# Two features of an output projection pinned behind the last attention score, and square sums of the last quarters moved between VectorE and GpSimd

## The chip, the cores and the metric

The kernel runs on one core of one Trainium2 chip. A core has TensorE (PE; its weight loads are listed apart as PEld), VectorE (DVE), ScalarE (ACT), GpSimd (POOL) and SyncE (SP, whose queue issues most transfers here). Each engine works through a queue of its own in order, and semaphores hold an instruction until those it depends on are done. The metric is device time in microseconds (us), as the median of several runs. Lower is better.

## The reference, cut to what matters

Two layers over 1024 latent tokens with 1024 features, with a prefix of 256 context tokens. The second layer, the only one that the change touches, is an odd layer: a conformer convolution (512 features) beside a neighbourhood attention (8 heads of 64), an output projection, a gated residual, and then the final norm:

```python
def odd_mixer(h_lat, h_ctx, w_in, w_out, ...):
    ...
    od = lax.map(d_row, (jnp.arange(rows), q_rows))          # neighbourhood attention
    od = jnp.moveaxis(od, 0, 1).reshape(bsz, n, D_W)
    y_lat = jnp.concatenate([oc, od * jax.nn.silu(dg)], axis=-1) @ w_out
    ...
x_lat = x_lat + g_l[:, None, :] * y_lat
return rms_norm(x_lat, final_g)      # x / sqrt(mean(x^2) + eps) * g
```

All values are 32-bit floats.

## The kernel before

**Products.** Every product of 32-bit data is made of three TensorE products: each operand is split in a high part (a cast on ScalarE, L312) and a low part (the rest, a subtraction on GpSimd or VectorE, L315), and `mm3` issues high by high (L332), high by low (L333) and low by high (L334). In names, `wh`/`wl` are the parts of a weight block, `wr` the block as it was transferred, `od` the parts of the gated attention output.

**Order.** The code is a set of generators. `weave` runs the attention (`main`) and lets steps of a second generator (`fill`) in between, in a ratio taken from the table `WV`. A scheduler then sets each engine's order from estimated times, and `tc.issue_after(x)` pins what is issued under it behind instruction `x`. So the order on an engine is not that of the code, and has to be read from the program.

**Attention of the second layer.** It is worked through in groups of one pair of heads by one half of the tokens (512). For each block of keys of a group: score (L509, L513, tile `st`), on most blocks the addition of a bias on VectorE (L518), exponential on ScalarE (L519 or, where there is no bias, L521; tile `pf`), split into `ph` and `pl`, and three products with the values (L460, L461, L462) that add up in `ov`. After the last block VectorE makes the reciprocal of the denominators (L470 transpose to `r`, L472, L473 transpose to `rb`), multiplies (L1337, tile `y`) and gates (L1339), and `y` is split once more (L312, L315) into the eighth block of 128 attention features of the output projection, `od` of that half. The last group belongs to the second half of the tokens. `sts` is the list of all score products; its last entry is the first score product (L509) of the last block.

**Output projection.** The 1024 inputs of the projection are eight blocks f = 0 to 7 of 128; f = 0 to 3 come from the convolution, f = 4 to 7 from the attention. Outputs are eight blocks too (e = 0 to 7, "features" below), for the two halves of tokens. What is ready early is added early: `out1_part` makes the product of the given blocks `fs` for halves `ks` and adds it, times the gate, to the residual (L1409, `x` += `po` * `modT`). It goes over pairs of features (`e2`), whose weights it loads first (`load_w`: transfer, cast, split). One call is for f = 4, 5, 6 of the second half (k = 1): per feature, nine products of 512 columns. `out1_end(k)` finishes a stretch of tokens: k = 0 is the first half (f = 4 to 7), k = 1 and k = 2 are the third and the fourth quarter (256 columns each, f = 7 alone).

**Square sums and norm.** For each finished feature `out1_end` squares it on ScalarE (L1438). The squares of e = 0 and 1 are the two accumulators, and those of e = 2 to 7 are added to them (L1442): even ones to the first, odd ones to the second. The table `SQP` says per k which of these adds run on GpSimd; the others run on VectorE. For k = 2 the two accumulators are added too (L1445). `rstd_steps` sums them over partitions on TensorE (L259, `trs`), adds epsilon (L262, `rbv`), takes the power -1/2 on GpSimd (L246, `nr`) with one refining step on VectorE (L247 to L249), and spreads the result over partitions (L269, `bc`). `final_norm` copies that to SBUF (L1453, `bcs`) and scales the features: those in `FNP[k]` on ScalarE and GpSimd (L1457, L1458), the others on VectorE (L1460), and sends pairs of them out (L1462).

Of the kernel before, what the change touches and what calls it, by code (L numbers as in the profile page):

```python
# [54 lines left out]
LAG = (6, 6, 6, 12)  # L55
FIN = (2, 2)
WV = (77, 45, 85, 24, 12)
# [4 lines left out]
ADDS = (0, 0, 1)  # L62
BCT = ("mx", "st", "mx")
FNP = ((0, 1, 2, 3, 4, 5, 6), (0, 2, 4, 6), (6,))
SQP = ((2, 3, 4, 5, 6), (), (4, 6))
ENDS = ((0, 0, 512), (1, 0, 256), (1, 256, 256))
LATE = 100
GB = 2
# [20 lines left out]
def tile_kernel(ctx: ExitStack, tc: tile.TileContext, a, out):  # L89
# [12 lines left out]
    sts = []  # L102
# [169 lines left out]
    @contextmanager  # L272
    def later(n):

        p = tc.cur_priority
        tc.cur_priority = p + n
        yield
        tc.cur_priority -= n

    def run(gen):  # L280

        while True:
            try:
                next(gen)
            except StopIteration as e:
                return e.value
# [255 lines left out]
    def weave(main, nmain, fill, nfill, last=True, all_fill=True, lag=0):  # L542

        done = 0
        for k in range(nmain):
            next(main, None)
            while done * nmain < (k + 1) * nfill:
                with ExitStack() as cx:
                    cx.enter_context(later(FL[layer[0]]))
                    if lag and len(sts) >= lag:  # L550
                        cx.enter_context(tc.issue_after(sts[-lag].ins))
                    next(fill, None)
                done += 1
        if all_fill:
            for _ in fill:
                pass
        if last:
            for _ in main:
                pass
# [133 lines left out]
    with ExitStack() as p0x:  # L693
# [208 lines left out]
        main = attn_gen(a0, [group0(u, qb) for u in ORDER for qb in QORD], VS0, LOOK0)  # L902
# [117 lines left out]
    with ExitStack() as l1x:  # L1020
# [357 lines left out]
        def x2_load(e):  # L1378
            for c in range(2):
                x2_of[e, c] = half("xs", "hf")  # L1380
                SC.dma_start(x2_of[e, c], X1[:, e, c * 512 : (c + 1) * 512])

        def od_load(hf):
            od[hf] = bigp.tile([P, 2, 3, 512], F32R, tag="big", name=nm("od"))
            for f in range(3):
                split(yo[:, f, hf], od[hf][:, 0, f, :], od[hf][:, 1, f, :], "s", ODE)
# [21 lines left out]
                x = x2[k][:, e, o : o + n]  # L1408
                VE.scalar_tensor_tensor(x, pp, scale, x, op0=ALU.mult, op1=ALU.add)  # L1409

        def out1_part(fs, ks=(0, 1)):
            for e2 in range(4):
                w = load_w(wp, a["od_wo"], e2, 256, WB, dks=fs)
                for e in (2 * e2, 2 * e2 + 1):
                    if fs[0] == 0:
                        x2_load(e)
                    for k in ks:
                        yield from out1(fs, e, k, *w)
# [3 lines left out]
        def out1_end(k):  # L1422
# [3 lines left out]
            for e in range(DK):  # L1426
# [14 lines left out]
                else:  # L1441
                    (GP if e in SQP[k] else VE).tensor_tensor(accs[e % 2], accs[e % 2], sq, op=ALU.add)  # L1442
                yield
# [24 lines left out]
        def ends(evs):  # L1468
            for ev in evs:
                k = int(ev[1])  # L1470
                if ev[0] == "e":
                    yield from out1_end(k)
                elif ev[0] == "c":
                    bcs[k] = yield from rstd_steps(dpool, sums[k], ENDS[k][2], BCT[k])
                else:
                    yield from final_norm(k, bcs[k])

        main = attn_gen(dlow, groups1, VSH, LOOK1, {11: [], 12: [13, 14], 13: [15]})
# [4 lines left out]
        assert fin[0] >= 12  # L1483
        for hf in (1, 0):
            od_load(hf)
        weave(main, WV[3], out1_part((4, 5, 6), (1,)), 8, False, True, LAG[3])
        assert fin[0] >= 14
        weave(main, WV[4], ends(EV0), NEV, False, True)
        wend = load_end(wp, a["od_wo"], 7, 256, WB)
        run(main)  # L1490
        solo[0] = True
        run(ends(EVS))


# [120 lines left out]
```

## Time and profile before

| | |
|---|---|
| median of three runs | 1559.18 us (1559.18, 1565.87, 1557.75) |
| the profiled execution | 1559.91 us, of which the trace's span is 1558.1 us |
| busy share of the span | PE 94%, PEld 75%, DVE 67%, ACT 48%, POOL 51% |
| mean granted TensorE clock | 0.965 |
| the chain that ended last, by engine | PE 79%, DVE 13%, DMA 3% |

The page of the profile gives the busy time of each engine, the costliest groups of instructions, and the chain of work that ended last, followed back from the last instruction. TensorE is the busiest engine and carries most of the chain. Shares over the whole span hide that the end of the program looks different; its stretches are shown with the prediction. A row of the timeline gives start and duration in us, engine, line, operation, output and inputs by name, shape, and in brackets the idle time before it and what ended that.

### The profile page before, as it was taken

To read this page: it belongs to the slowest core of one execution; us is meant where nothing else is said; L and a number is where in the kernel's file an instruction comes from. 1 tells how busy PE (TensorE), PEld (TensorE's weight loads), DVE (VectorE), ACT (ScalarE), POOL (GpSimd) and SP (SyncE) were. 2 spreads that over 40 slices of the span, in tenths; PEclk is the share of its full clock that TensorE was granted. 3 is DMA by queue.
4 is the path that set the end of the run, shared out by engine and by line. 5 is a ranking of instruction groups with operands and counts; after the bars stand their busy time and mean duration, and the time that the engine had idled before them with its cause. 6 is when DMAs were issued, how large, how long until landed. Compare 5 with 4: busy or idle time off the path is not lost.

```text
span 1558.1 us, 21469 instructions
## 1 busy us (share of the span) xinstructions
PE 1459.1 (94%) x7084; PEld 1175.6 (75%) x7084; DVE 1050.0 (67%) x2113; ACT 746.9 (48%) x1418; POOL 801.5 (51%) x637
## 2 busy tenths in 40 slices
PE   6899999998998989999999878999999899989995
PEld 2786978896896768876866657888887688868875
DVE  2833557579579765466677846999756566577866
ACT  3721434444435564447556663443334355455563
POOL 3530434455445765557656664665632344364675
PEclk9899999999999999999999889999999899999996
DMA  9473315422312245121112012111445777878632
GB/s 366 161 244 124 108 57 181 143 70 92 119 51 79 92 151 177 54 68 50 51 31 92 7 34 86 58 55 41 142 159 192 216 204 236 263 227 243 183 111 108
DMA packets 154168, 199.83 MB, mean 128 GB/s; under 512 B 14716, under 2 KB 95816, under 8 KB 154056
## 3 DMA queue, kind: packets, MB, share of 16 engines
q1 hardware_dynamic: 147392, 186.88, 38.0%
q10 hardware_dynamic: 6664, 11.57, 2.3%
q8 instruction: 56, 0.92, 0.2%
q14 instruction: 56, 0.46, 0.1%
HBM read 148.07 MB, written 49.02 MB: 126 GB/s over the span
## 4 chain that ended last, share of the span: by engine, by line
PE 79%; DVE 13%; DMA 3%; issue 2%; ACT 2%; POOL 1%; SPq 0%; DVEq 0%; POOLq 0%; ACTq 0%
PE p L332 7%; PE p L333 7%; PE p L334 7%; PE ov L460 4%; PE ov L462 4%; PE ov L461 4%; PE st L509 4%; PE st L513 4%; PE po L333 4%; PE po L332 4%; PE po L334 4%; PE pq L332 3%; PE pq L334 3%; PE pq L333 3%; PE pm L184 2%
## 5 line engine op out<-in xcount | busy, mean ns | idle before, releaser
L315 POOL TENSOR_TENSOR pl<-pf,ph 128x512 fp32r<-128x512 f32 (+4 forms) x321 | 396.8, 1247 | 375.8 <-ACT ph L312 328.7
L521 ACT ACTIVATE pf<-st 128x512 f32<-128x512 f32 x284 | 166.3, 597 | 210.3 <-PE st L513 171.0
L315 POOL TENSOR_TENSOR wl<-wr,wh 128x512 fp32r<-128x512 f32 (+2 forms) x131 | 170.5, 1313 | 141.4 <-ACT wh L312 121.4
L312 ACT CAST ph<-pf 128x512 fp32r<-128x512 f32 (+4 forms) x364 | 209.2, 588 | 29.0 <-PE ov L461 16.7
L332 PE MATMUL p<-hh,wh 128*128 128x512 f32 x448 | 178.2, 398 | 5.3 <-ACT hh L312 2.8
L333 PE MATMUL p<-hl,wh 128*128 128x512 f32 x448 | 176.1, 394 | 0.6 <-POOL hl L315 0.6
L334 PE MATMUL p<-hh,wl 128*128 128x512 f32 x448 | 173.7, 394 | 0.0
L509 PE MATMUL st<-QH,KAt 128*128 128x512 f32 (+4 forms) x364 | 140.9, 388 | 8.9 <-ACT pf L521 8.1
L460 PE MATMUL ov<-ph,Vt 128*128 128x512 f32 (+4 forms) x364 | 142.5, 392 | 5.6 <-DVE y L670 4.3
L462 PE MATMUL ov<-pl,Vt 128*128 128x512 f32 (+4 forms) x364 | 141.9, 390 | 1.8 <-POOL pl L315 1.8
L461 PE MATMUL ov<-ph,Vt 128*64 128x512 f32 (+4 forms) x364 | 140.5, 386 | 0.0
L513 PE MATMUL st<-QL,KBt 68*128 68x512 f32 (+4 forms) x364 | 136.4, 386 | 2.0 <-DVE QL L438 2.0
L1085 DVE SCALAR_TENSOR_TENSOR cps<-U,taps,cps 128x512 f32<-128x512 f32 x184 | 126.4, 751 | 0.9
L312 ACT CAST wh<-wr 128x512 fp32r<-128x512 f32 (+2 forms) x134 | 81.2, 613 | 92.3 <-DMA wr<-in_od_d_dram 19.1
L332 PEld LDWEIGHTS p<-hh,wh 128*128 128x128 f32 x448 | 85.1, 190 | 23.8 <-ACT hh L312 3.0
L333 PEld LDWEIGHTS p<-hl,wh 128*128 128x128 f32 x448 | 85.2, 190 | 18.7 <-POOL hl L315 1.7
L334 PEld LDWEIGHTS p<-hh,wl 128*128 128x128 f32 x448 | 85.1, 190 | 17.5
L633 DVE TENSOR_REDUCE mp<-mx 128x1 f32<-128x512 f32 x128 | 85.2, 681 | 17.4 <-PE mx L632 16.5
L332 PE MATMUL pq<-wh,hh 128*128 128x384 f32 x256 | 88.4, 345 | 2.8 <-ACT hh L312 2.8
L509 PEld LDWEIGHTS st<-QH,KAt 128*128 128x128 f32 x364 | 69.7, 192 | 26.5 <-ACT pf L521 11.9
L954 DVE SCALAR_TENSOR_TENSOR x<-po,modT,x 128x512 f32<-128x512 f32 (+1 forms) x72 | 47.0, 657 | 62.1 <-PE po L334 61.7
L333 PE MATMUL pq<-wl,hh 128*128 128x384 f32 x256 | 87.4, 342 | 0.0
(280 smaller groups left out, 3470.8 us busy)
## 6 DMA issues: line engine op xcount, KB each, us to landing
mw<-in_mod_w_dram SPq DMA_DIRECT2D x16, 1024.0 KB, 5.5
Q<-qs SPq DMA_DIRECT2D x40, 256.0 KB, 2.2
QH<-Q SPq DMA_DIRECT2D x80, 128.0 KB, 2.7
mw<-in_mod_w_dram SPq DMA_DIRECT2D x16, 512.0 KB, 6.7
wr<-in_od_d_dram SPq DMA_DIRECT2D x32, 256.0 KB, 3.2
wr<-in_ev_qkv_dram SPq DMA_DIRECT2D x16, 384.0 KB, 5.2
KAt<-KD SPq DMA_DIRECT2D x16, 384.0 KB, 5.9
wr<-in_od_wo_dram SPq DMA_DIRECT2D x22, 256.0 KB, 3.3
```

Of the source, the lines that this page charges most:

```text
L312: acts.append(SC.copy(hi, src))
L315: (GP if leng == "g" else VE).tensor_tensor(lo, src, hi.bitcast(F32), op=ALU.subtract)
L332: PE.matmul(o, lh, rh, start=first, stop=False)
L333: PE.matmul(o, lh, rl, start=False, stop=False)
L334: PE.matmul(o, ll, rh, start=False, stop=last)
L460: PE.matmul(o, V[:, 64:192], ph[:, :n], start=(t == 0), stop=False)
L461: PE.matmul(g.ov[0:64, q0 : q0 + n], V[:, 0:64], ph[:, :n], start=False, stop=False)
L462: PE.matmul(o, V[:, 64:192], pl[:, :n], start=False, stop=(last and g.sink is None))
L509: sts.append(PE.matmul(st[:, :n], KA[:, cs], g.QH[:, q0 : q0 + n], start=True, stop=False))
L513: PE.matmul(st[:, :n], KB[0:68, cs], g.QL[0:68, q0 : q0 + n], start=False, stop=True)
L521: acts.append(SC.activation(pf[:, :n], st[:, :n], AF.Exp, scale=1.0 if g.bias else SCALE))
L1085: VE.scalar_tensor_tensor(pc, uc, w, pc, op0=ALU.mult, op1=ALU.add)
```

## The change

It has two parts. In the projection of blocks 4 to 6 for the second half, the last pair of features (e2 = 3, e = 6 and 7) leaves the weave and is issued after the attention has been run, pinned behind the last score product. And `SQP` changes: in the third quarter the adds of e = 3, 5, 7 go from VectorE to GpSimd; in the fourth quarter GpSimd gets e = 3 and 5 in place of e = 4 and 6.

```diff
-SQP = ((2, 3, 4, 5, 6), (), (4, 6))
+SQP = ((2, 3, 4, 5, 6), (3, 5, 7), (3, 5))
...
-        def out1_part(fs, ks=(0, 1)):
-            for e2 in range(4):
+        def out1_part(fs, ks=(0, 1), es=range(4)):
+            for e2 in es:
                 w = load_w(wp, a["od_wo"], e2, 256, WB, dks=fs)
...
-        weave(main, WV[3], out1_part((4, 5, 6), (1,)), 8, False, True, LAG[3])
+        weave(main, WV[3], out1_part((4, 5, 6), (1,), range(3)), 6, False, True, LAG[3])
         assert fin[0] >= 14
         weave(main, WV[4], ends(EV0), NEV, False, True)
         wend = load_end(wp, a["od_wo"], 7, 256, WB)
         run(main)
         solo[0] = True
+        with tc.issue_after(sts[-1].ins):
+            run(out1_part((4, 5, 6), (1,), (3,)))
         run(ends(EVS))
```

What the scheduler makes of it is shown at three places. Names carry the tile's number, which differs between the two programs.

On TensorE, around the last score product, before. `po_3770` is the last feature (e = 7) of the first half, twelve products, of which the last two rows are shown; `st_15453` is the last score; `trs_15560` are the column sums of the first half.

```order
L333 MATMUL po_3770_15527<-od_3241_13684,wh_15502 128x512
L334 MATMUL po_3770_15527<-od_3241_13684,wl_15503 128x512
L509 MATMUL st_15453<-QH_14550,KAt_11662 128x512
L513 MATMUL st_15453<-QL_14551,KBt_11661 128x512
L460 MATMUL ov_15314<-ph_15301,Vt_11665 128x512
```

```order
L461 MATMUL ov_15314<-ph_15456,Vt_11665 64x512
L259 MATMUL trs_15560<-ones,sq_3733_15373 128x2
L259 MATMUL trs_15560<-ones,sq_3727_15344 128x2
L259 MATMUL trs_15560<-ones,sq_3733_15373 128x2
L259 MATMUL trs_15560<-ones,sq_3727_15344 128x2
L259 MATMUL trs_15560<-ones,sq_3733_15373 128x2
L259 MATMUL trs_15560<-ones,sq_3727_15344 128x2
L259 MATMUL trs_15560<-ones,sq_3733_15373 128x2
L462 MATMUL ov_15314<-pl_15457,Vt_11665 128x512
L269 MATMUL bc_15577<-ident,nr_15571 128x128 x4
L332 MATMUL po_3788_15615<-od_3243_13686,wh_15604 128x256
```

The same place after. `st_15419` is the last score, `po_3762` the twelve products of the first half's last feature, `po_3786` and `po_3787` the moved features.

```order
L462 MATMUL ov_15280<-pl_15242,Vt_11665 128x352
L509 MATMUL st_15419<-QH_14550,KAt_11662 128x512
L513 MATMUL st_15419<-QL_14551,KBt_11661 128x512
L460 MATMUL ov_15280<-ph_15267,Vt_11665 128x512
L461 MATMUL ov_15280<-ph_15267,Vt_11665 64x512
L462 MATMUL ov_15280<-pl_15268,Vt_11665 128x512
L460 MATMUL ov_15280<-ph_15315,Vt_11665 128x320
L461 MATMUL ov_15280<-ph_15315,Vt_11665 64x320
L462 MATMUL ov_15280<-pl_15316,Vt_11665 128x320
L332 MATMUL po_3762_15493<-od_14963,wh_15462 128x512
```

```order
L461 MATMUL ov_15280<-ph_15422,Vt_11665 64x512
L259 MATMUL trs_15526<-ones,sq_3719_15310 128x2
L332 MATMUL po_3786_15593<-od_14956,wh_15582 128x512
L333 MATMUL po_3786_15593<-od_14956,wh_15582 128x512
L462 MATMUL ov_15280<-pl_15423,Vt_11665 128x512
L332 MATMUL po_3787_15604<-od_14956,wh_15582 128x512
```

The moved products follow the last score, and the twelve of the first half's last feature, which stood ahead of it, now follow it as well. Two of the moved stand ahead of the last L462, the other sixteen behind it; then come the other seven `trs`, fifteen products of 256 columns, and only then `bc`.

On VectorE, from the last gating (L1339) to the first norm's steps, before:

```order
L1442 TENSOR_TENSOR sq_3733_15373<-sq_3733_15373,sqt_15557 128x512
L262 TENSOR_SCALAR rbv_15569<-trs_15560 128x4
L470 STREAM_TRANSPOSE r_3771_15543<-ov_15314 64x256 x2
L472 RECIPROCAL r_3772_15544<-r_3771_15543 128x8
L247 TENSOR_TENSOR nt_15572<-nr_15571,rbv_15569 128x4
L473 STREAM_TRANSPOSE rb_15545<-r_3772_15544 128x256
L248 SCALAR_TENSOR_TENSOR nt_15572<-nt_15572,nr_15571 128x4
L1337 TENSOR_TENSOR y_3774_15550<-ov_15314,rb_15545 64x256 x2
L249 SCALAR_TENSOR_TENSOR nr_15571<-nt_15572,nr_15571 128x4
L1339 SCALAR_TENSOR_TENSOR y_3774_15550<-y_3774_15550,gt_3718_15308 64x512
L315 TENSOR_TENSOR od_3243_13686<-y_3774_15550,od_3243_13686 64x512
```

And after:

```order
L1337 TENSOR_TENSOR y_3766_15516<-ov_15280,rb_15511 64x256 x2
L1339 SCALAR_TENSOR_TENSOR y_3766_15516<-y_3766_15516,gt_3710_15274 64x512
L1409 SCALAR_TENSOR_TENSOR x_3242_13685<-po_3786_15593,modT_103,x_3242_13685 128x512
L1409 SCALAR_TENSOR_TENSOR x_3242_13685<-po_3787_15604,modT_103,x_3242_13685 128x512
L315 TENSOR_TENSOR od_3243_13686<-y_3766_15516,od_3243_13686 64x512
L262 TENSOR_SCALAR rbv_15535<-trs_15526 128x4
L1409 SCALAR_TENSOR_TENSOR x_3242_13685<-po_3792_15629,modT_103,x_3242_13685 128x256
L1409 SCALAR_TENSOR_TENSOR x_3242_13685<-po_3794_15637,modT_103,x_3242_13685 128x256
L247 TENSOR_TENSOR nt_15538<-nr_15537,rbv_15535 128x4
```

The two accumulations of the moved features stand between y and od's low part, and `rbv` with the steps behind it has moved from before `y` to behind that low part.

On GpSimd, from the last `pl` on, before and then after; `sq_3791` is the odd accumulator of the third quarter, `sq_3810` and `sq_3812` the even and the odd one of the fourth:

```order
L315 TENSOR_TENSOR pl_15457<-pf_15458,ph_15456 128x512
L246 TENSOR_TENSOR nr_15571<-rbv_15569,mhalf 128x4
L1458 TENSOR_TENSOR x_3240_13683<-x_3240_13683,bcs_15582 128x512 x7
L1442 TENSOR_TENSOR sq_3810_15698<-sq_3810_15698,sq_3818_15728 128x256
L1442 TENSOR_TENSOR sq_3810_15698<-sq_3810_15698,sq_3822_15744 128x256
L246 TENSOR_TENSOR nr_15684<-rbv_15682,mhalf 128x2
```

```order
L315 TENSOR_TENSOR pl_15423<-pf_15424,ph_15422 128x512
L315 TENSOR_TENSOR wl_15583<-wr_15581,wh_15582 128x512
L315 TENSOR_TENSOR wl_15589<-wr_15587,wh_15588 128x256
L246 TENSOR_TENSOR nr_15537<-rbv_15535,mhalf 128x4
L1458 TENSOR_TENSOR x_3240_13683<-x_3240_13683,bcs_15548 128x512 x7
L1442 TENSOR_TENSOR sq_3791_15627<-sq_3791_15627,sq_3795_15642 128x256
L1442 TENSOR_TENSOR sq_3812_15705<-sq_3812_15705,sq_3816_15720 128x256
L1442 TENSOR_TENSOR sq_3791_15627<-sq_3791_15627,sq_3799_15658 128x256
L1442 TENSOR_TENSOR sq_3812_15705<-sq_3812_15705,sq_3820_15736 128x256
L1442 TENSOR_TENSOR sq_3791_15627<-sq_3791_15627,sq_3803_15674 128x256
L246 TENSOR_TENSOR nr_15684<-rbv_15682,mhalf 128x2
```

Two splits of the moved weights have come in ahead of the power, and five adds stand behind the seven scalings where two stood.

## The prediction

> **What bounds the kernel now.** I read first the table of stretches over the last 118 us (columns: start and end, length, then busy time and count of TensorE's products and weight loads, VectorE, ScalarE and GpSimd, the granted TensorE clock, DMA share and GB/s).
>
> ```profile
> 1465.00:1489.30 24.30, 24.30 (x122) 20.38 (x122) 18.32 (x36) 12.17 (x24) 17.08 (x16) 1.00 0.59 178
> 1489.30:1500.30 11.00, 9.63 (x47) 7.10 (x45) 10.38 (x25) 6.81 (x14) 5.14 (x5) 1.00 0.53 158
> 1500.30:1522.50 22.20, 22.20 (x107) 18.52 (x106) 13.65 (x25) 17.93 (x35) 18.41 (x16) 1.00 0.18 51
> 1522.50:1531.50 9.00, 6.11 (x37) 5.24 (x37) 5.08 (x14) 2.24 (x4) 2.84 (x3) 0.76 0.00 0
> 1531.50:1546.90 15.40, 10.39 (x58) 9.49 (x57) 14.44 (x31) 8.77 (x22) 11.77 (x10) 0.72 0.35 137
> ```
>
> TensorE is busy for all of the first and the third stretch; in the second it idles 1.37 of 11.00 us while VectorE works 10.38. From the last score (1522.5) on, no engine is full until VectorE takes 14.44 of 15.40 us. So there are two regimes: a TensorE queue that ends with the last score, and a tail in which the engines hand work to each other. The timeline gives the points of hand-over (start, duration, engine, line, operation).
>
> ```profile
> 1505.03 0.39 PE L509 MATMUL st<-QH,KAt 128*128 128x512 f32 x1
> 1519.38 0.40 PE L332 MATMUL po<-od,wh 128*128 128x512 f32 x1
> 1521.88 0.39 PE L334 MATMUL po<-od,wl 128*128 128x512 f32 x1
> 1522.33 0.40 PE L513 MATMUL st<-QL,KBt 68*128 68x512 f32 x1
> 1524.47 1.28 POOL L315 TENSOR_TENSOR pl<-pf,ph 128x512 fp32r<-128x512 f32 x1 [1.43 <-ACT ph L312]
> 1526.48 0.48 PE L462 MATMUL ov<-pl,Vt 128*128 128x512 f32 x1
> 1526.66 0.16 DVE L262 TENSOR_SCALAR rbv<-trs 128x4 f32<-128x4 f32 x1 [2.05 <-PE trs L259]
> 1526.90 1.03 POOL L246 TENSOR_TENSOR nr<-rbv,mhalf 128x4 f32<-128x4 f32 x1 [1.16 <-DVE rbv L262]
> 1527.00 0.92 DVE L470 STREAM_TRANSPOSE r<-ov 64x256 f32<-64x256 f32 x2 [0.18 <-PE ov L462]
> 1529.79 0.69 DVE L1339 SCALAR_TENSOR_TENSOR y<-y,gt 64x512 f32<-64x512 f32 x1
> 1529.81 2.08 PE L269 MATMUL bc<-ident,nr 128*128 128x128 f32 x8 [2.85 <-DVE nr L249]
> 1531.16 0.69 DVE L315 TENSOR_TENSOR od<-y,od 64x512 fp32r<-64x512 f32 x1 [0.68 <-ACT od L312]
> 1532.64 9.47 POOL L1458 TENSOR_TENSOR x<-x,bcs 128x512 f32<-128x512 f32 x7 [4.72 <-ACT bcs L1453]
> ```
>
> Read it as two strands. The last head's output needs the last score, its exponential and the low part (pl, ready at 1525.75), then L462, r to y on VectorE, and od's low part at 1531.85. The first half's norm needs its column sums (trs), rbv, GpSimd's power, bc; then GpSimd multiplies seven features of that half (L1458), from 1532.64 to 1542.11. The end:
>
> ```profile
> 1542.71 0.41 DVE L1442 TENSOR_TENSOR sq<-sq,sq 128x256 f32<-128x256 f32 x1
> 1542.87 1.75 PE L259 MATMUL trs<-ones,sq 128*128 128x2 f32 x8
> 1544.02 1.61 POOL L1442 TENSOR_TENSOR sq<-sq,sq 128x256 f32<-128x256 f32 x2 [1.91 <-ACT sq L1438]
> 1545.58 0.89 POOL L246 TENSOR_TENSOR nr<-rbv,mhalf 128x2 f32<-128x2 f32 x1
> 1546.54 0.42 DVE L1445 TENSOR_TENSOR sq<-sq,sq 128x256 f32<-128x256 f32 x1
> 1547.11 0.99 PE L259 MATMUL trs<-ones,sq 128*128 128x2 f32 x4 [2.49 <-DVE nt L247]
> 1549.20 0.37 ACT L1453 COPY bcs<-bc 128x256 f32<-128x256 f32 x1 [3.32 <-PE bc L269]
> 1550.97 0.37 ACT L1453 COPY bcs<-bc 128x256 f32<-128x256 f32 x1 [1.40 <-PE bc L269]
> 1549.60 4.60 DVE L1460 SCALAR_TENSOR_TENSOR x<-x,fg,bc 128x256 f32<-128x256 f32 x11
> ```
>
> The third quarter's sums are complete about 1543 (its trs starts at 1542.87, eight products in 1.75 us) and the last quarter's at 1546.96 (L1445; four products of trs in 0.99). From complete sums to the scale in SBUF the last quarter took 1550.97 - 1546.96 = 4.01 us; the first scaling starts 0.40 after the first scale, at 1549.60, runs to 1554.20, and 3.9 us later the span ends at 1558.1. Of the adds of squares:
>
> ```profile
> L1442 DVE TENSOR_TENSOR sq<-sq,sq 128x256 f32<-128x256 f32 x10 | 7.3, 732 | 0.1
> L1442 POOL TENSOR_TENSOR sq<-sq,sq 128x256 f32<-128x256 f32 x2 | 1.5, 730 | 2.1 <-ACT sq L1438 1.9
> ```
>
> The sum is made against this execution (1559.91 us, 0.73 above the median of 1559.18); the shift is then put on the median.
>
> **The change, term by term.**
>
> *What leaves the TensorE queue.* The 18 products of the two pinned features go behind the last score, and so do the 12 of the first half's last feature, which the scheduler placed ahead of it before. Those twelve run from 1519.38 to 1521.88, 0.227 apart; thirty are 6.8 us. Nine of them leave before the second stretch, where VectorE is the bound: what TensorE gains ahead of it, about 2.0 us (9 x 0.227), shows there as idle time, since VectorE's work has not shrunk. It passes on only what the head before arrives earlier; I take 0.2 to 0.3 of the 2.0 and lose 1.8. In the two full stretches the rest is real: the last score ends 6.8 - 1.8 = 5.0 earlier, at about 1517.7 instead of 1522.73. Ends: all 6.8, or, if VectorE's stretch swallows twice as much, 3.2.
>
> *What now stands between the last score and L462.* Before, pl was ready at 1525.75 and L462 began at 1526.48, behind the trs. Now the twelve products and two of the moved stand there (14 x 0.227 = 3.2 us), with eleven ov of the group (five of 512 columns, three of 320, three of 224: 1.9 us by that spacing scaled with the columns) and one trs: some 5.3 us, more than the 3.0 us that pl takes after the last score. So TensorE decides: r starts about 1523.1, not 1527.00: 3.9 earlier. The weights of the moved products must be there by 1522.5, or L462 waits with them, 1 to 1. Their transfers wait for buffers that the splits of the weights before them free; the one on GpSimd is the first row here, the second is the page's (KB, us to landing).
>
> ```profile
> 1513.72 1.74 POOL L315 TENSOR_TENSOR wl<-wr,wh 128x512 fp32r<-128x512 f32 x1
> wr<-in_od_wo_dram SPq DMA_DIRECT2D x22, 256.0 KB, 3.3
> ```
>
> Even at the time of before, 1515.5 and 3.3 us for the transfer give 1518.8, so I cost them at nothing. Their two casts on ScalarE and two splits on GpSimd (1.3 and some 0.7 us) fall into idle time there: GpSimd idles 4.72 us ahead of L1458 (its row above) and does only the power in between. Ahead of that power they would count only beyond 1528.8; they end near 1523.
>
> *VectorE behind y.* r to the end of y took 1530.48 - 1527.00 = 3.48 with three small steps of the norm (0.12 to 0.17 each) among them; without these, about 3.2: y is ready at 1526.3. TensorE's 16 remaining moved products need 3.6 us behind L462, so the first of the two new accumulations (L1409, 128x512) can begin about 1526.6. Both stand ahead of od's low part:
>
> ```profile
> 1522.31 0.75 DVE L1409 SCALAR_TENSOR_TENSOR x<-po,modT,x 128x512 f32<-128x512 f32 x1 [2.07 <-PE po L334]
> ```
>
> They cost 2 x 0.7, and the low part ends at 1526.6 + 1.4 + 0.7 = 1528.7, 3.15 earlier than 1531.85.
>
> *The norm of the first half.* rbv now stands behind that low part, so at 1528.8 instead of 1526.66: 2.1 later. Before, rbv to bc took 3.15 us (1526.66 to 1529.81); now power (1.03), two accumulations of 256 columns among the small steps, and 15 products of 256 columns ahead of bc on TensorE. Those products were 0.21 apart at first and 0.12 later:
>
> ```profile
> 1533.18 0.41 PE L333 MATMUL po<-od,wh 128*128 128x256 f32 x1
> 1533.39 0.41 PE L334 MATMUL po<-od,wl 128*128 128x256 f32 x1
> 1535.33 0.28 PE L333 MATMUL po<-od,wh 128*128 128x256 f32 x1
> 1535.45 0.28 PE L334 MATMUL po<-od,wl 128*128 128x256 f32 x1
> ```
>
> So 1.8 to 3.2 us from 1528.7: bc at about 1531.2. From bc to the first L1458 took 2.83, with bc at the slow clock of its stretch (0.76); between 2.0 and 2.83 I take 2.4. L1458 starts at 1533.6 instead of 1532.64, and the lead is gone on this strand. Ends: 1531.8 (all of the 1.8 us kept) and 1534.8 (15 products at 0.21 and bc at 2.83).
>
> *GpSimd's adds.* Five adds (three of the third quarter, two of the last, where there were two in all) stand behind the seven L1458, in order, so they can't start before 1533.6 + 9.47 = 1543.1. The price of one: 0.73 in the group above, 0.8 in the pair's row (1.61 for two). I take 0.77: the fifth ends at 1543.1 + 3.85 = 1546.9. The lower end is 0.73; the upper end 1.1, the row of a VectorE add beside L1458:
>
> ```profile
> 1537.05 1.10 DVE L1442 TENSOR_TENSOR sq<-sq,sq 128x256 f32<-128x256 f32 x1
> ```
>
> The Trainium skill, SBUF — State Buffer, section Who interferes with whom, says that a VectorE instruction with two SBUF inputs contends with a GpSimd instruction that reads SBUF, one blocking the other; the trace agrees (a VectorE add 1.10 beside L1458, 0.41 after it). By it the five adds on GpSimd also block VectorE's four of the last quarter, a push of up to 1 us the same way as the sum.
>
> The third quarter's column sums, which had been ready at about 1543, wait for that fifth add. With the template of the last quarter it is 4.01 us from there to the scale, and 0.5 more for eight products of trs instead of four (7 of 8 x 1.75 = 1.5 against 0.99), and 0.40 to the first scaling: 1546.9 + 4.9 = 1551.8 instead of 1549.60, 2.2 later. Break-even is a fifth add that ends at 1544.7. The last quarter's own sums come at about 1547.0 (fourth GpSimd add, a VectorE add of 0.41, L1445 of 0.42): as before, so it isn't the bound. The eleven scalings and the output transfers behind are unchanged.
>
> *What VectorE saves.* Three of its ten adds, 3 x 0.73 = 2.2 us of 14.44. It waits for GpSimd at the end, so I cost this at nothing. Lost cover: ScalarE's squares of the last quarter reuse buffers that GpSimd's adds free, so they come after 1543.9, one each add; the fourth is ready before VectorE's last add needs it.
>
> **The sum.** Gain at r 3.9, at od's low part 3.15, at L1458 -1.0, at the first scaling -2.2: 1559.91 + 2.2 = 1562.1 in this execution, on the median 1559.18 + 2.2 = 1561.4 us.
>
> **The rivals.**
>
> *The lead arrives in part (faster).* For it: TensorE is full in 46.5 us of the stretches ahead of the last score, and VectorE, the busiest engine of the tail, loses 2.2 us of work. It needs L1458 at 1531.8, its seven at 1.29 (first row below) and adds at 0.73: 1531.8 + 9.03 + 3.65 = 1544.5, 0.2 before break-even; with power and bc 1 us quicker than I have them, 1.2. Time 1558.0 to 1559.0. Against it: rbv's place behind od's low part, and GpSimd's order. The full 3.15 (1556.0) would need the fifth add at 1541.5, before L1458 ends.
>
> ```profile
> 1508.85 1.29 POOL L315 TENSOR_TENSOR wl<-wr,wh 128x512 fp32r<-128x512 f32 x1
> 1515.43 1.74 POOL L1442 TENSOR_TENSOR sq<-sq,sqt 128x512 f32<-128x512 f32 x1
> ```
>
> *GpSimd's stretch swells (slower).* Beside a busy VectorE a GpSimd operation of 512 columns took 1.74 instead of 1.29 (rows above). With L1458 starting at 1534.8, its seven at 1.5 (10.5) and five adds at 1.1 (5.5), the fifth ends at 1550.8, 6.1 past break-even: 1565.3; with half of what these add, 1548.8 and 1563.3. It decides once the fifth add ends after 1547.7, 3 us past break-even. For it: VectorE's accumulations and remaining adds fall into the same stretch. Against: L1458 ran beside such adds before (the one at 1537.05) and took 9.47 / 7 = 1.35 each.
> The Trainium skill, GPSIMD Engine Reference, section 4.1 Engine selection, gives elementwise adds of two inputs to VectorE, with GpSimd about 2 times slower; the trace agrees when nothing else reads (0.73 to 0.8 against 0.41), and by that rule, at 0.82 an add, the fifth would end 0.25 us later than in the sum.
>
> *Nothing arrives.* The strands cancel within 0.5 us: 1559.2. For it: the terms at L1458 and at the adds rest on bounds 3 us apart; I count it with the likeliest.
>
> **How the numbers follow.** Likeliest, from no shift to +3.2 us (1559.2 to 1562.4): 0.52, taken at 1561.4. The lead in part (1556.0 to 1559.2): 0.23. GpSimd's stretch swells (1562.4 to 1566): 0.21. Else 0.04. The range cuts the outer part of each rival: 1556.5 to 1565.5. About 0.5%, or 7.8 us, is what a measurement of this kernel can tell from no change (the three runs span 1557.75 to 1565.87). No case of gain reaches it, since all thirty products are 6.8 us: faster 0.02. Slower needs more than the whole swollen stretch, 6.1: 0.05. Same 0.93.
>
> **What would show it.** The last score ends near 1517.7 and r starts near 1523.1 (else the first two terms are wrong); rbv directly after od's low part, near 1528.8; the first L1458 near 1533.6; five GpSimd adds in one block that ends near 1546.9, and the first 256-column L1460 near 1551.8. The prediction is wrong if L1458 starts well before 1532, if the adds take 0.5 or 1.1, if the weights of the moved products hold L462, or if the second stretch gives back none of TensorE's lead or all of it.

## The result, and the profile after

The change made the kernel slower: 1566.05 us (median of 22 runs, 1561.77 to 1571.48) against 1561.57 us of the kernel before (22 runs 1555.22 to 1566.95). The ratio is 1.0033, 95% interval [1.0022, 1.0043], some 5.2 us. The prediction had a loss of 2.2 us and 1561.4 us; 1566.05 lies just outside its range (1556.5 to 1565.5). Of the 4.65 us between the two, 2.4 are the kernel before itself, whose median was 1559.18 in the three runs then known and is 1561.57 in 22; the other 2.3 are the change's loss, sized too low (the medians are 4.5 apart where 2.2 were forecast; the ratio gives 5.2 and the traces 5.0). The loss is clear of noise, but it is smaller than the 0.5% that the prediction asked for before it would call the kernel slower: its likeliest word, "same", holds.

The profiled execution of the changed kernel has a span of 1562.9 us, 4.8 above that of before. Executions drift against each other by some microseconds long before the first instruction that differs (the mark named here stands between 1449.9 and 1457.8 us in the fourteen traces), so positions are compared from a common mark: the first step (L470) of the reciprocal in the last group that is the same in both programs.

```profile
1452.74 0.92 DVE L470 STREAM_TRANSPOSE r<-ov 64x256 f32<-64x256 f32 x2
1452.57 0.92 DVE L470 STREAM_TRANSPOSE r<-ov 64x256 f32<-64x256 f32 x2
```

The first row is of before, the second of the changed kernel. The next rows are the changed kernel's timeline from the last score to the end, in the order in which the work hands over.

```profile
1518.06 0.40 PE L513 MATMUL st<-QL,KBt 68*128 68x512 f32 x1
1523.66 0.40 PE L462 MATMUL ov<-pl,Vt 128*128 128x512 f32 x1
1523.89 0.86 DVE L1442 TENSOR_TENSOR sq<-sq,sqt 128x512 f32<-128x512 f32 x1 [0.76 <-ACT sqt L1438]
1524.78 0.92 DVE L470 STREAM_TRANSPOSE r<-ov 64x256 f32<-64x256 f32 x2
1527.34 0.69 DVE L1339 SCALAR_TENSOR_TENSOR y<-y,gt 64x512 f32<-64x512 f32 x1
1528.06 1.41 DVE L1409 SCALAR_TENSOR_TENSOR x<-po,modT,x 128x512 f32<-128x512 f32 x2
1529.50 0.69 DVE L315 TENSOR_TENSOR od<-y,od 64x512 fp32r<-64x512 f32 x1
1530.22 0.16 DVE L262 TENSOR_SCALAR rbv<-trs 128x4 f32<-128x4 f32 x1
1533.38 1.91 PE L269 MATMUL bc<-ident,nr 128*128 128x128 f32 x8
1535.99 9.49 POOL L1458 TENSOR_TENSOR x<-x,bcs 128x512 f32<-128x512 f32 x7 [4.50 <-ACT bcs L1453]
1545.44 3.87 POOL L1442 TENSOR_TENSOR sq<-sq,sq 128x256 f32<-128x256 f32 x5
1549.37 1.44 PE L259 MATMUL trs<-ones,sq 128*128 128x2 f32 x6 [5.65 <-POOL sq L1442]
1554.10 4.40 DVE L1460 SCALAR_TENSOR_TENSOR x<-x,fg,bc 128x256 f32<-128x256 f32 x11 [0.47 <-ACT bcs L1453]
```

The chain is the one that the prediction drew. The last score ends 4.1 us earlier than before (counted from the mark: 65.89 against 69.99); by r 2.05 are left, by od's low part 1.5; rbv follows directly behind it. The first L1458 starts 3.5 us later than before (83.42 against 79.90), its seven take 9.49 where they took 9.47, the five adds stand behind them in one block, and the column sums of the third quarter wait for that block (the idle time of 5.65 before trs names it). The first scaling of a quarter comes 4.7 us later, the end of the span 5.0.

### The profile page after: what moved, and what is told of

Its sections match the earlier page's. It is cut to its first block, busy times and chain, and to the rows that moved or that the text cites. A ratio compares the mean times of both kernels' runs of the same rounds, so it can differ in the third digit from the quotient of the medians.

```text
span 1562.9 us, 21458 instructions
## 1 busy us (share of the span) xinstructions
PE 1458.7 (93%) x7084; PEld 1174.2 (75%) x7084; DVE 1047.3 (67%) x2110; ACT 746.4 (48%) x1418; POOL 805.1 (52%) x640
## 4 chain that ended last, share of the span: by engine, by line
PE 77%; DVE 12%; DMA 5%; issue 2%; POOL 2%; ACT 1%; SPq 0%; ACTq 0%; DVEq 0%; POOLq 0%
PE p L332 6%; PE p L333 6%; PE p L334 6%; PE ov L460 4%; PE ov L462 4%; PE ov L461 4%; PE po L332 4%; PE po L333 4%; PE po L334 4%; PE st L509 4%; PE st L513 4%; PE pq L332 3%; PE pq L334 3%; PE pq L333 3%; PE pg L332 2%
## 5 line engine op out<-in xcount | busy, mean ns | idle before, releaser
L462 PE MATMUL ov<-pl,Vt 128*128 128x512 f32 (+4 forms) x364 | 140.8, 387 | 1.7 <-POOL pl L315 1.7
```

The lines of the kernel that those rows point to most:

```text
L462: PE.matmul(o, V[:, 64:192], pl[:, :n], start=False, stop=(last and g.sink is None))
```

## The experiments

All of them start from one of the two kernels and change what is shown. The table has all positions in microseconds from the common mark of each execution's own trace, and the ratio to runs of the kernel before that were taken beside it, with its 95% interval.

| kernel | last score ends | r | od low ends | rbv | L1458 starts | ends | last GpSimd add ends | L1445 ends | first quarter scaling | span ends | ratio |
|---|---|---|---|---|---|---|---|---|---|---|---|
| before | 69.99 | 74.26 | 79.11 | 73.92 | 79.90 | 89.37 | 92.89 | 94.22 | 96.86 | 105.36 | |
| the change | 65.89 | 72.21 | 77.62 | 77.65 | 83.42 | 92.91 | 96.74 | 97.48 | 101.53 | 110.33 | 1.0033 [1.0022, 1.0043] |
| pin only | 66.56 | 72.88 | 78.29 | 78.32 | 84.08 | 93.77 | 97.83 | 98.57 | 99.96 | 111.85 | 1.0044 [1.0028, 1.006] |
| sums only | 69.99 | 74.26 | 79.11 | 73.92 | 79.88 | 89.33 | 93.39 | 94.12 | 98.17 | 107.48 | 1.0014 [0.9997, 1.0031] |
| pin behind trs | 65.79 | 70.96 | 76.17 | 74.83 | 81.87 | 91.23 | 95.29 | 96.03 | 100.07 | 108.55 | 1.002 [1.0007, 1.0032] |
| the same, old sums | 65.54 | 70.70 | 75.91 | 74.58 | 81.56 | 91.29 | 95.09 | 96.15 | 97.42 | 109.28 | 1.0025 [1.001, 1.004] |
| six scalings | 65.77 | 72.08 | 77.48 | 77.51 | 83.17 | 91.20 | 95.27 | 96.02 | 100.06 | 109.40 | 1.0033 [1.0019, 1.0046] |
| last add on GpSimd | 65.76 | 71.39 | 76.95 | 76.98 | 82.79 | 92.03 | 96.10 | 96.84 | 100.88 | 109.46 | 1.0023 [1.0011, 1.0035] |
| pin only, norm first | 66.59 | 72.91 | 78.31 | 78.34 | 84.10 | 93.77 | 97.82 | 98.57 | 103.13 | 111.41 | 1.0039 [1.0022, 1.0056] |
| pin four | 60.98 | 68.66 | 75.11 | 75.13 | 79.65 | 88.78 | 93.76 | 94.88 | 97.75 | 106.27 | 1.0006 [0.9991, 1.0021] |
| pin behind bc | 66.57 | 71.74 | 76.95 | 75.61 | 80.42 | 89.20 | 94.38 | 95.99 | 98.19 | 106.71 | 1.0004 [0.9989, 1.0018] |
| four behind bc | 59.48 | 67.16 | 72.37 | 71.03 | 75.84 | 84.59 | 96.95 | 98.02 | 100.57 | 109.10 | 1.0031 [1.0014, 1.0048] |
| six | 58.78 | 66.46 | 72.91 | 72.94 | 77.68 | 86.46 | 98.86 | 99.93 | 102.57 | 111.13 | 1.0042 [1.0029, 1.0055] |
| six behind bc | 58.44 | 66.12 | 71.33 | 69.99 | 74.80 | 83.49 | 103.81 | 105.97 | 108.60 | 117.10 | 1.0085 [1.007, 1.01] |

The last columns agree: what the span's end has moved against before (105.36), divided by 1560, is the ratio to within its interval in every row. But each row is one trace, and the interval is some 1.5 us to either side. How far a single trace can be trusted shows in the first column: eight kernels have the same 300 TensorE products between the mark and the last score, and in five of them that score ends at 65.5 to 65.9, in three (pin only, pin only with the norm first, pin behind bc) at 66.6. So a difference of less than about 1 us between two rows is read here only along the steps that lead to it, and stays a reading of one trace.

### One part alone

The pin alone:

```diff
-SQP = ((2, 3, 4, 5, 6), (3, 5, 7), (3, 5))
+SQP = ((2, 3, 4, 5, 6), (), (4, 6))
```

> The pin as in the change, the square sums divided between VectorE and GpSimd as before. Theory (GpSimd's queue sets the end: start of the seven L1458, then its adds, then the quarters' norms): L1458 still starts near 1536.0, 3.3 us later than before, but only two adds stand behind it and the third quarter's sums don't wait for them; GpSimd is done with both near 1547.5 to 1548, and the time is 1 to 2 us above before, 2.5 to 3.5 below the changed kernel. Rival B (the pin alone is the loss, by VectorE's longer way to od's low part and to the quarters): 4 to 5 us above before, equal to the changed kernel. Rival C (the adds on GpSimd are the loss, by themselves): no slower than before, up to 1.7 us faster, since od's low part is that much earlier.

Measured: 6.5 us above before in the trace, ratio 1.0044. My theory (1 to 2) fell, and rival B, that the pin by itself is the loss, came nearest. In the trace it is even 1.5 us slower than the whole change, of which 0.7 is there at the last score already; the ratios can't tell the two apart. L1458 is late as expected. What I had not seen are the two rows in which VectorE and GpSimd then stand. The table of stretches, first the changed kernel, then the pin alone, each over the ten microseconds in which L1458 runs:

```profile
1536.83:1546.83 10.00, 4.40 (x24) 3.73 (x23) 7.54 (x15) 4.95 (x13) 10.00 (x10) 0.76 0.45 175
1538.41:1548.41 10.00, 6.02 (x29) 4.49 (x27) 10.00 (x16) 5.24 (x13) 9.51 (x7) 0.78 0.37 145
```

In the changed kernel GpSimd is full (10.00) and VectorE at 7.54; with the old division VectorE is full and GpSimd nearly so. The last quarter's sums (L1445) end later with the old division, 98.57 against 97.48. And its norm is held up a second time, by order: GpSimd's rows at the end of the pin alone show the power of the last quarter behind the four scalings of the third.

```profile
1554.15 2.77 POOL L1458 TENSOR_TENSOR x<-x,bcs 128x256 f32<-128x256 f32 x4 [2.17 <-ACT bcs L1453]
1556.87 0.71 POOL L246 TENSOR_TENSOR nr<-rbv,mhalf 128x2 f32<-128x2 f32 x1
1559.48 0.37 ACT L1453 COPY bcs<-bc 128x256 f32<-128x256 f32 x1 [5.41 <-PE bc L269]
```

The new division of the sums alone:

```diff
-SQP = ((2, 3, 4, 5, 6), (), (4, 6))
+SQP = ((2, 3, 4, 5, 6), (3, 5, 7), (3, 5))
```

> Only the division of the square sums as in the change, the two features not pinned. Theory: L1458 starts at 1532.6 as before and ends at 1542.1, five adds of 0.77 follow, the fifth ends near 1546.0 and the first scaling of the third quarter is at 1550.8 instead of 1549.6: 1 to 1.5 us above before. Less than the two parts together (4.5), because in before GpSimd stood idle for 1.9 us ahead of its adds and either part uses that up. Rival B: within 0.5 us of before. Rival C: 4 to 5 us above before.

```profile
1533.40 9.45 POOL L1458 TENSOR_TENSOR x<-x,bcs 128x512 f32<-128x512 f32 x7 [4.69 <-ACT bcs L1453]
1542.81 4.10 POOL L1442 TENSOR_TENSOR sq<-sq,sq 128x256 f32<-128x256 f32 x5
1551.69 4.40 DVE L1460 SCALAR_TENSOR_TENSOR x<-x,fg,bc 128x256 f32<-128x256 f32 x11 [0.47 <-ACT bcs L1453]
```

As the theory said: L1458 not moved, the adds behind it, the first scaling 1.3 us later. The span's end is 2.1 later (the ratio's interval still holds 1); the other 0.8 lies behind the last scaling, in the last transfers (4.9 us from its end to the span's end, 3.9 in before), and no run separates why. In the traces the two parts don't add: 6.5 and 2.1 alone, 5.0 together. Without the pin the new division costs 2.1; with it, it saves 0.8 beyond what the last score accounts for. The pair with the pin behind trs, below, has the same sign (0.7). The timing alone would not show it.

### What of the pin costs

If the cost is what the pin puts ahead of the first norm, moving it behind that norm must take it away. First only behind the column sums (`tsums` collects the trs products):

```diff
-        with tc.issue_after(sts[-1].ins):
+        with tc.issue_after(tsums[-1].ins):
             run(out1_part((4, 5, 6), (1,), (3,)))
```

> The change, but the two features are pinned behind the last column sum (trs) of the first half's norm instead of the last score: on TensorE the eighteen products stand behind the trs, on VectorE rbv stands ahead of od's low part again. Theory: rbv near 1528, L1458 starts at 1531.5 to 1532.7, the fifth add ends at 1544.8 to 1546.1; 0 to 1.2 us above before, 3.3 to 4.5 below the changed kernel. Rival C: as the changed kernel, 4 to 5 us above before, since the five adds are the same.

> As the kernel with the pin behind the trs, and the square sums divided as before. Theory: both losses are taken away and TensorE's lead is left: L1458 as early as before or up to 1 us earlier, od's low part 2 us earlier, so VectorE's stretch of the quarters starts earlier: 1 to 2.5 us faster than before. Rival B: 2 to 4 us above before, since the moved products and their two accumulations still stand among the tail's work.

The first came out between the theories, 3.2 us above before, the second at 3.9, where the rival had it. rbv did come early (74.83), but bc did not, and that was my error: the eighteen products now stood between trs and bc on TensorE. The norm's last refining step (L249) is done at 1530.41, and bc follows 3.3 us later; eight of the products ahead of it are 0.43 us apart, the others 0.23.

```profile
1530.25 0.16 DVE L249 SCALAR_TENSOR_TENSOR nr<-nt,nr 128x4 f32<-128x4 f32 x1
1526.30 1.72 PE L259 MATMUL trs<-ones,sq 128*128 128x2 f32 x14 [1.74 <-DVE sq L1442]
1533.70 1.05 PE L269 MATMUL bc<-ident,nr 128*128 128x128 f32 x8
1535.52 9.36 POOL L1458 TENSOR_TENSOR x<-x,bcs 128x512 f32<-128x512 f32 x7 [5.76 <-ACT bcs L1453]
```

So, behind bc (`bcm` collects its products):

```diff
-        with tc.issue_after(sts[-1].ins):
+        with tc.issue_after(bcm[-1].ins):
             run(out1_part((4, 5, 6), (1,), (3,)))
```

> The change (two features, the new division of the sums), but pinned behind bc, the broadcast of the first half's norm, instead of the last score: on TensorE the eighteen products stand behind bc, on VectorE both accumulations behind od's low part and the norm's steps. Theory, as it stands after the run with four features (work that goes between the last score and bc delays L1458 and with it the end; work that goes behind bc lies beside L1458 and costs little): L1458 starts 3.5 to 4.5 us earlier than in the changed kernel, at or up to 1 us before its time in before; the end within 1.5 us of before, 3.5 to 6 below the changed kernel. Rival (the two accumulations and the products cost their time wherever they stand in the tail): 2.5 us or more above before.

Here the theory held: the same two features, the same division of the sums, and the time is that of before (ratio 1.0004 [0.9989, 1.0018]; 1.35 us above it in the trace). L1458 starts 3.0 us earlier than in the changed kernel, and the end is 3.6 earlier, although the last score came 0.7 later.

```profile
1529.03 0.92 DVE L470 STREAM_TRANSPOSE r<-ov 64x256 f32<-64x256 f32 x2 [0.49 <-PE ov L462]
1529.98 0.69 DVE L1442 TENSOR_TENSOR sq<-sq,sqt 128x512 f32<-128x512 f32 x1
1537.71 8.78 POOL L1458 TENSOR_TENSOR x<-x,bcs 128x512 f32<-128x512 f32 x7 [3.54 <-ACT bcs L1453]
```

This is the run that shows the place of the moved work, not its amount and not the adds, as the main cause. It is not the only thing that differs: the scheduler has also put r ahead of the add of squares (the first two rows; also with the pin behind trs), which in the changed kernel stands ahead of r. The run on that add, below, has it at 0.9 us, so most of the 3.6 is left for the place of the moved work. The pin behind trs divides the way: with the accumulations behind rbv but the products still ahead of bc, L1458 is 1.55 earlier than in the changed kernel (some 0.6 of it is the add), and with both behind bc another 1.45. It isn't a gain either: L1458 starts at 80.42, no earlier than before.

### GpSimd's queue

One scaling fewer on GpSimd:

```diff
-FNP = ((0, 1, 2, 3, 4, 5, 6), (0, 2, 4, 6), (6,))
+FNP = ((0, 1, 2, 3, 4, 5), (0, 2, 4, 6), (6,))
```

> The changed kernel with six instead of seven of the first half's scalings on GpSimd (the feature e = 6 goes to VectorE). Theory (GpSimd's queue, L1458 and then the five adds, sets the end): L1458 ends 1.35 us earlier, the adds and the first scaling follow; the end is 1.0 to 1.4 us earlier than in the changed kernel, 3.6 to 4 above before. Rival (VectorE sets the end of the tail): it gets one more scaling of 0.75, so 0.5 to 0.8 us later than the changed kernel. Counted from the reciprocal near 1452.6, which stands ahead of all differences.

```profile
1540.37 8.03 POOL L1458 TENSOR_TENSOR x<-x,bcs 128x512 f32<-128x512 f32 x6 [4.40 <-ACT bcs L1453]
1548.37 4.10 POOL L1442 TENSOR_TENSOR sq<-sq,sq 128x256 f32<-128x256 f32 x5
```

The six take 8.03 instead of 9.49, the adds and the first scaling come 1.5 earlier and the end 0.9 (110.33 to 109.40), on the side of the theory, that GpSimd's queue sets the end of the changed kernel. The timing can't tell 0.9 us (1.0033 again), so this rests on the one trace, in which L1458's shorter row and the rows behind it account for the move.

### The add ahead of r

In the changed kernel a 128x512 add of the first half's squares stands on VectorE just ahead of r and ends 0.7 us after L462's result is there. On GpSimd instead:

```diff
-SQP = ((2, 3, 4, 5, 6), (3, 5, 7), (3, 5))
+SQP = ((2, 3, 4, 5, 6, 7), (3, 5, 7), (3, 5))
```

> The changed kernel with the last odd add of the first half's squares (128x512, 0.86 us on VectorE just ahead of r) on GpSimd. Theory: r starts when L462 is done, 0.5 to 0.7 us earlier, and y, od's low part, rbv and all behind them by as much: the end 0.5 to 0.7 us earlier than in the changed kernel. Rival: the column sums wait for the add on GpSimd and rbv isn't earlier: no change, or up to 1 us later.

```profile
1526.23 0.92 DVE L470 STREAM_TRANSPOSE r<-ov 64x256 f32<-64x256 f32 x2 [0.96 <-PE ov L462]
```

r now waits for L462 alone, starts 0.8 earlier counted from the mark, od's low part and L1458 are 0.7 and 0.6 earlier, and the end 0.9. That is the theory's size, in one trace; the ratio (1.0023 against 1.0033) can't tell it.

### The last quarter's norm

The pin with the old division, and the scalings of the third quarter pinned behind the norm's steps of the fourth (`steps` collects the power and the last refining step):

```diff
-EVS = "e1 c1 e2 f1 c2 f2".split()
+EVS = "e1 c1 e2 c2 f1 f2".split()
...
-                    GP.tensor_tensor(x, x, bcs, op=ALU.mult)
+                    with tc.issue_after(steps[-2]) if k == 1 else ExitStack(): GP.tensor_tensor(x, x, bcs, op=ALU.mult)
...
-                    VE.scalar_tensor_tensor(x, x, fg[:, e : e + 1], bc[:, :n], op0=ALU.mult, op1=ALU.mult)
+                    with tc.issue_after(steps[-1]) if k == 1 else ExitStack(): VE.scalar_tensor_tensor(x, x, fg[:, e : e + 1], bc[:, :n], op0=ALU.mult, op1=ALU.mult)
```

> The pin with the square sums divided as before, as in the first of these runs, but with the scalings of the third quarter (on GpSimd and on VectorE) put behind the norm's steps of the fourth. Theory: what made the pin alone 1.5 us slower than the whole change is that the fourth quarter's rbv and power stood behind the third quarter's scalings: its scale came 6.8 us after its sums, and comes 4.0 to 4.5 after them now; the end is 1 to 2 us earlier than with the pin alone, 4.5 to 5.5 above before, so that the new division of the sums costs nothing on top of the pin. Rival: the five adds on GpSimd are a loss of their own: 2 us or more below the changed kernel, 3 or less above before.

Only 0.4 us came back, not 1 to 2, in two traces whose last scores end at the same place (66.56 and 66.59): the last scale comes 5.95 us after L1445 instead of 6.76, where I had expected 4.0 to 4.5, and the third quarter's scalings, which had been early, now wait for it. So the order of the last norm explains little of the pin's cost; L1445 at 98.57, 4.35 us later than before, explains most of it.

### More of it

> The change with four features pinned instead of two (36 products, four accumulations, two more loads of weights). Theory: each pair costs TensorE 4.1 us and VectorE 1.4 us behind the last score and brings less than 4.1 ahead of it, since VectorE's stretch there gives nothing and the clock goes down where TensorE idles: 3 to 6 us above the changed kernel, 8 to 11 above before. Rival (the lead is paid one to one): within 1 us of the changed kernel.

```diff
-        weave(main, WV[3], out1_part((4, 5, 6), (1,), range(3)), 6, False, True, LAG[3])
+        weave(main, WV[3], out1_part((4, 5, 6), (1,), range(2)), 4, False, True, LAG[3])
...
-            run(out1_part((4, 5, 6), (1,), (3,)))
+            run(out1_part((4, 5, 6), (1,), (2, 3)))
```

The theory of that time, that each pair costs more than it brings, was wrong by its sign: four pinned features are as fast as before (1.0006), 4 us faster than two. The second pair takes another 4.9 us off the last score's end, and the scheduler puts its products behind bc, so that between score and bc there still stands only one pair, while its weights are still split ahead of L1458:

```profile
1526.42 1.96 POOL L315 TENSOR_TENSOR wl<-wr,wh 128x512 fp32r<-128x512 f32 x2 [3.54 <-ACT wh L312]
1531.72 1.05 PE L269 MATMUL bc<-ident,nr 128*128 128x128 f32 x8
1532.53 0.47 PE L332 MATMUL po<-od,wh 128*128 128x512 f32 x1
```

It is this run that led to the pin behind bc. More still, in the same way with six features, and with four and six behind bc:

> Six features pinned behind the last score as in the change. In TensorE's order one pair of them stands ahead of the column sums and two pairs behind bc. Theory: the last score 3 to 5 us earlier than with four, and what stands between it and bc is one pair, as with two and four: the end 2 to 5 us below the run with four, 1 to 4 below before. Rival (the lead is used up in stretches where VectorE is the bound): the end as with four, within 1 us of before or above it.

> Four features pinned behind bc. Theory: the last score 4 to 5 us earlier than with two, L1458 as much earlier; but the second pair's weight splits stand behind the seven L1458 on GpSimd, so that pair's products wait for these; the end 0 to 4 us below before. Rival (that wait decides): 0 to 3 us above before.

> Six features pinned behind bc. Theory: as with six behind the last score, and 1 to 2 us less, since no moved product stands ahead of bc; but four weight splits stand behind L1458 on GpSimd: 1 to 5 us below before if that wait is covered, 0 to 3 above if it is not.

All three were slower than before (1.0042, 1.0031, 1.0085), on the rivals' side, and both pins behind bc by more than these had it. L1458 did start 2 to 5 us earlier than before (77.68, 75.84, 74.80), but the adds behind it no longer follow it. GpSimd's rows with six behind bc:

```profile
1532.60 8.69 POOL L1458 TENSOR_TENSOR x<-x,bcs 128x512 f32<-128x512 f32 x7 [3.54 <-ACT bcs L1453]
1541.24 1.95 POOL L315 TENSOR_TENSOR wl<-wr,wh 128x512 fp32r<-128x512 f32 x2
1547.10 1.99 POOL L315 TENSOR_TENSOR wl<-wr,wh 128x512 fp32r<-128x512 f32 x2 [3.91 <-ACT wh L312]
1555.79 0.73 POOL L1442 TENSOR_TENSOR sq<-sq,sq 128x256 f32<-128x256 f32 x1 [6.71 <-ACT sq L1438]
```

The weights of the later pairs are split behind L1458, then their products, accumulations and squares follow, and GpSimd idles 6.71 us for the first square to add. VectorE idles as well, for the first product behind such a split:

```profile
1547.27 1.41 DVE L1409 SCALAR_TENSOR_TENSOR x<-po,modT,x 128x512 f32<-128x512 f32 x2 [8.80 <-PE po L334]
```

So, as far as the traces show, it is not a full engine that sets the end there but a hand-over: a split of weights that stands behind the seven L1458 in GpSimd's queue, and all that waits for it; no run moves the splits alone. With four behind bc and with six behind the last score, one pair's splits stand there (GpSimd then idles 5.97 and 6.01 us for the squares), with six behind bc two; with four behind the last score none does, and that kernel is as fast as before. None of the versions tried is measurably faster than the kernel before.

## Why the prediction was wrong, step by step

**The direction and the chain were right.** Lead on TensorE, spent on the way to L1458; GpSimd's L1458 and five adds in a block; the third quarter's norm behind the fifth add. The adds cost 3.87 us (forecast 3.85), L1458 9.49 (9.47), and from the fifth add to the first scaling it took 4.79 (4.9). Behind the start of L1458 the sum was right to 0.1 us.

**What failed is the sum ahead of L1458**, forecast 1.0 us later than before and measured 3.5. Counted from the mark and put on the time of before, L1458 starts at 1536.2; even the upper end, 1534.8, missed it, since it varied the norm's terms alone and left r where the forecast had it. Four terms were mis-sized, all on one side (the differences counted from the mark):

- *The last score's lead*, forecast 5.0, was 4.1. The stretch where VectorE is the bound did not only keep what TensorE gained there, as I had it; more was lost, and in it TensorE slowed down. The changed kernel's row of that stretch has a granted clock of 0.84, where before has 1.00, and products of 512 columns from 1495.4 on are 0.4 to 0.6 us apart; towards its end they are 0.22 to 0.24 apart again. That the slower clock is what took the 0.9 is not shown by a run of its own, but where the clock fell further in that place the last score came later still (last section).

```profile
1489.30:1500.30 11.00, 9.33 (x39) 6.91 (x38) 9.39 (x23) 6.85 (x15) 4.77 (x6) 0.84 0.46 129
```

```profile
1491.99 0.41 PE L509 MATMUL st<-QH,KAt 128*128 128x320 f32 x1 [1.10 <-DVE pf L518]
1495.42 0.80 PE L509 MATMUL st<-QH,KAt 128*128 128x512 f32 x1
1496.02 0.63 PE L513 MATMUL st<-QL,KBt 68*128 68x512 f32 x1
1496.44 1.05 PE L332 MATMUL po<-od,wh 128*128 128x512 f32 x2
1499.36 0.39 PE L509 MATMUL st<-QH,KAt 128*128 128x512 f32 x1
1499.58 0.40 PE L513 MATMUL st<-QL,KBt 68*128 68x512 f32 x1
```

- *r behind the last product*: forecast to start when L462 is done, it waited 0.7 us for the VectorE add of the first half's squares, which before was done 2.4 us ahead of it. The lead had brought r forward onto that add. The run with the add on GpSimd has r that much earlier.
- *From rbv to bc*, forecast 2.4, it took 3.16. The norm's last step (L249) was done at 1532.58, and bc waited 0.8 us more for TensorE, which had not finished the fifteen products ahead of it. They were not only TensorE work: one of them waits 0.34 us for an accumulation on VectorE, which stands among the norm's small steps, and from 1531.8 on they are 0.21 us apart or more, where most of those before were 0.12:

```profile
1531.32 0.39 PE L332 MATMUL po<-od,wh 128*128 128x256 f32 x1 [0.34 <-DVE x L1409]
1532.43 0.15 DVE L249 SCALAR_TENSOR_TENSOR nr<-nt,nr 128x4 f32<-128x4 f32 x1
1532.57 0.58 PE L332 MATMUL po<-od,wh 128*128 128x256 f32 x1
1533.16 0.41 PE L334 MATMUL po<-od,wl 128*128 128x256 f32 x1
```

- *From bc to L1458*, forecast 2.4, it took 2.61.

The lead's 0.9, the add's 0.7, the 0.8 on the way to bc and the last 0.2 add up to 2.6, against the 2.5 us by which L1458 was later than forecast; what else differs (L462 0.2 later, r to od's low part 0.2 shorter) cancels.

**What failed besides is the starting point**: a median of three runs that span 8 us stood for the kernel before, and 22 runs put it 2.4 us higher. With 1561.57 in its place the same sum and range would have read 1563.8 and 1558.9 to 1567.9. So it is by this, too, that the time lies outside the range, and the 2.2 us of shift would still have been less than half of the 5 that the traces and the ratio show.

**The rivals.** The swollen stretch of GpSimd ended near the measured time (1563.3 to 1565.3) but not by its mechanism: L1458 took 1.36 each and an add 0.77. The partial lead did not show, and the strands did not cancel. The price of an add behind L1458 was 0.77 us on GpSimd. On VectorE the same adds took 0.41 alone (before) and 0.41 to 1.27 beside L1458 (the changed kernel). The Trainium skill's rule (GPSIMD Engine Reference, section 4.1 Engine selection), about 2 times slower on GpSimd, had led to an estimate of 0.82; here GpSimd was not the dearer place by that factor as long as L1458 ran.

**What the prediction did not consider** is that the two parts of the change act on one another. It put both on one chain and added. In the traces the new division is a loss by itself (2.1 us) and a small gain once the pin has delayed the quarters' work (0.8), because with the old division VectorE is then the full engine (10.00 of 10.00 us in the table of stretches above). In the sum it was on the path either way, so this is not what made the forecast too small.

## What to carry to other kernels

Work that is pinned "behind the last product" goes into the hand-over that follows, and what counts there is whether it stands ahead of or behind the next engine's start: with the same eighteen products and two accumulations the kernel was 5.0 us above before when they stood ahead of a norm's broadcast, and 1.35 when they stood behind it. The same goes for the weights' splits, as the traces with four and six features behind bc read: behind GpSimd's long row they held up what followed. Before work is taken out of a queue, look at what else sets each stretch: where another engine is the bound, taking work away buys idle time, and on TensorE idle time was followed by a lower clock (0.84 here). And when a wait moves earlier, look for what it now meets: here a small add that had not been in the way. And a median of a few runs is part of a forecast: here it was half of the miss.

## What the runs showed of the hardware

Short idle times were followed by half of TensorE's pace. In the changed kernel idle gaps of 0.43, 0.21, 1.10 and 0.37 us within 5 us (2.1 in all) were followed by some three microseconds in which 512-column products stood 0.38 to 0.60 apart instead of 0.23. In before, gaps of 0.33, 0.33 and 0.67 us within 5 us (1.3 in all) in the same stretch had no such effect (1.00). No run changes these gaps alone. How much is lost differs between executions: of the eight traces with two pinned features, which have the same work up to there, five had a granted clock of 0.86 in the 12 us from 36.5 after the mark and the last score's end at 65.5 to 65.9, and three (the pin only, the same with the norm first, the pin behind bc) 0.72 and 66.6. With the pin behind bc the first of the moved products show the step itself. They follow the eight small products of bc, ahead of which TensorE had idled 2.43 us:

```profile
1534.88 2.08 PE L269 MATMUL bc<-ident,nr 128*128 128x128 f32 x8 [2.43 <-DVE nr L249]
1537.61 0.63 PE L334 MATMUL po<-od,wl 128*128 128x512 f32 x1
1538.03 0.63 PE L332 MATMUL po<-od,wh 128*128 128x512 f32 x1
1541.16 0.39 PE L332 MATMUL po<-od,wh 128*128 128x512 f32 x1
1541.39 0.40 PE L333 MATMUL po<-od,wh 128*128 128x512 f32 x1
```

They stand 0.43 apart up to 1540.2 and 0.23 from 1540.5 on. The Trainium skill (TensorE: Matmul & The Clock Gate, section What's actually happening) has the clock go to half after an idle window of about 3.4 us and back after one of sustained work, on a window that runs freely; the return 3.8 us after the first of the moved products (1536.61) fits; on the way down, no single gap in the changed kernel's stretch was longer than 1.10 us, so here the drop did not need an idle window of that length.
